# Writing four of eight memory steps of an encoder layer at another place in the instruction order

## The chip, the cores and the metric

The kernel runs on one core of a Trainium2 chip. The metric is the device time of one execution in microseconds (us). Before the change the median of three runs is 3056.3 us (3049.87 to 3058.04). One further execution was profiled; the profile's rows come from that one.

A core has five engines that run side by side, each with its own queue of instructions that it takes in order: TensorE (PE, matrix products; its weight loads are listed as PEld), VectorE (DVE), ScalarE (ACT), GpSimd (POOL) and SyncE (SP, which here only issues transfers). Transfers are carried out by 16 DMA engines that all queues share. The working memory is SBUF; products land in PSUM, from which ScalarE or VectorE copy them.

## The reference

One layer on a sequence of 2048 tokens with 1024 channels, all in 32-bit floats:

```
u    = rmsnorm(x);  P = u @ w_in                       # 1024 x 3600
hyena = long convolutions of P's first 1536 columns    # by FFT, two orders, gated
mlstm = two-way recurrence over q, k, v, o, gates      # 4 heads x 128
h    = x + concat(norm(hyena), norm(mlstm)) @ w_out
h    = h + cross_attention(rmsnorm(h), rmsnorm(mem))   # mem: 256 tokens, 4 heads x 256
h    = h + relu(rmsnorm(h) @ ff_w1)^2 @ ff_w2
out  = rmsnorm(h)
```

What matters here is the cross attention. Its scores are `(xn @ wq) . (memn @ wk)` and its output `softmax(scores) @ (memn @ wv) @ wo`, per head. The kernel forms two small matrices per head from the memory alone: `wq_h @ (memn @ wk_h)^T`, stored in DRAM as `gd` (the key step), and `(memn @ wv_h) @ wo_h`, stored as `vw` (the value step). Four heads make four key steps and four value steps. Attention later multiplies the tokens with `gd` and the softmax with `vw`, and reads both from DRAM.

## The kernel before

Tokens are taken in two halves of 1024 (`hf` 0 and 1), whose operands lie in SBUF as a high and a low part (`xh`, `xl`); a product is three matmuls of such parts (`mm3`, lines 355 to 359). The input projection consists of *sweeps* (`sweep`, 256 columns of `w_in` each, transposed result, then a width-3 convolution; columns 0 to 5 feed Hyena, 6 and 7 are q, 8 and 9 are k) and of *natural blocks* (`natural`, 256 columns, tokens in rows; blocks 0 and 1 are v, 2 and 3 are o and the gates). Each sweep and natural block takes its weights from one stream, `self.wst`, whose order is the list `items` in `inproj_open`. The stream loads one entry ahead, into tiles `wh` and `wl` of which there are two each, through smaller staging tiles `wn`, and splits them on ScalarE and VectorE (`split`, line 366).

`program` writes the instructions in this order. First come the sweeps 0 to 3 of half 0 and of half 1, woven with the generation of Hyena's filters. Then `rest` is woven with `hyena`: `weave(rest, p.hyena(hs), 445, 329)` lets both generators advance in the ratio of 445 to 329, measured by the numbers that they yield. `rest` holds the sweeps 4 to 9 of half 1, the natural blocks 3, 0, 1, 2 of half 1, and then the blocks and sweeps of half 0, among which the gate computation (`gates`) and the backward states of the recurrence (`states`) are advanced. The last ones are the sweeps 6 and 7 and the natural block 2 of half 0. Hyena has for each of two orders a forward transform (`spectrum`, writes `zs`), 16 steps (lines 956, 987, 1030: read `fs` and `zs`, write `zg` by POOL's queue), and a last stage of eight blocks, which reads `zg` and the gate rows of `hy` (lines 339 and 974) and multiplies them with small products (lines 173 and 186).

When both are through, the tiles `xh` and `xl` are given up (`turned_in`), and the memory steps (`memproj`) are written: eight times a projection (`project`, line 708, 32 products in the records) and a key or value step (line 725 or 737), of which each projection stands one step ahead. After the first projection the first five steps of the recurrence (`mlstm`) are written among them. The memory, transposed and scaled with its norm, comes from `prep_mem`, which also begins the loads of the memory weights (`raw_stream`, unsplit, up to four entries ahead). Results go from PSUM to staging tiles `st` (three, shared with sweeps and natural blocks) on ScalarE and to DRAM by POOL's queue. Then comes attention, woven with the other steps of the recurrence, and the feed-forward part.

The written order isn't the final one: the builder orders each engine's instructions itself by an estimate of their times (`schedule_with_timeline_sim=True`), with the written order as priority, except where a line pins instructions to it.

Of the kernel before, what the change touches and what calls it, by code (L numbers as in the profile page):

```python
# [128 lines left out]
class Prog:  # L129
# [249 lines left out]

    def weights(self, pool, w, n, kc=4, bufs=2, nbufs=2, pin=False):  # L380
        nc = self.nc
        kt = w.shape[0] // 128
        hi = pool.tile([128, kt, n], F32R, tag="wh", name="wh", bufs=bufs)
        lo = pool.tile([128, kt, n], F32R, tag="wl", name="wl", bufs=bufs)
        if n > 512:
            for k0 in range(kt):
                for c0 in range(0, n, 512):
                    cs = slice(c0, c0 + 512)
                    nat = self.isw.tile([128, 512], F32, tag="wn", name="wn", bufs=nbufs)
                    nc.sync.dma_start(out=nat, in_=w[128 * k0:128 * k0 + 128, cs])  # L390
                    self.split(hi[:, k0, cs], lo[:, k0, cs], nat)
            return hi, lo
        for k0 in range(0, kt, kc):
            nat = self.isw.tile([128, kc, n], F32, tag="wn", name="wn", bufs=nbufs)
            nc.sync.dma_start(out=nat, in_=w[128 * k0:128 * (k0 + kc), :].rearrange("(k p) c -> p k c", p=128))
            self.split(hi[:, k0:k0 + kc], lo[:, k0:k0 + kc], nat, pin)
        return hi, lo

    def stream(self, pool, items, cur, **kw):
        for w, n in items:  # L400
# [25 lines left out]
    def inproj_open(self, es):  # L426
        nc, tc, a = self.nc, self.tc, self.a
        self.d_hy = self.dram("hy", (3, L, CH))
        self.d_qt = self.dram("qt", (4, 128, L))
        self.d_kt = self.dram("kt", (4, 128, L))  # L430
        self.d_kn = self.dram("kn", (L, CH))
        self.d_vd = self.dram("vd", (L, CH))
        self.d_od = self.dram("od", (L, CH))
        self.d_gt = self.dram("gt", (L, 16))
        sw = self.isw = es.enter_context(tc.tile_pool(name="i_w", bufs=1))
        for tag, n, bufs in (("cv", 1088, 2), ("wn", 544, 4)):
            for _ in range(bufs):
# [24 lines left out]

# [202 lines left out]
    def prep_mem(self):  # L665
# [24 lines left out]
                yield  # L690
        self.prepq = halves()

    def memproj(self):
        nc, sb = self.nc, self.isb
        gd = self.dram("gd", (2, 128, 8, 512))
        vw = self.dram("vw", (4, 128, 8, 256))
        self.pop(2)
        mt = self.memt

        mul = nc.tensor.matmul  # L700

        def project():
            w = next(self.mst)
            p = self.mm().rearrange("p (k t) -> p k t", k=2)
            for m in range(2):
                ms = slice(128 * m, 128 * m + 128)
                for k in range(8):
                    mul(p[:, m], w[:, k, ms], mt[k // 4][:, k % 4], start=k == 0, stop=k == 7)
            t = sb.tile([128, 4, 256], F32, tag="xn", name="kt", bufs=2)[:, 0:2]
            nc.scalar.copy(t, p)  # L710
            return t

        def staged(p):
            o = self.ist.tile([128, 2, 256], F32, tag="st", name="o", bufs=3)
            nc.scalar.copy(o, p)
            return o

        def keys(h, t):
            q = next(self.mst)
            for i2 in range(4):  # L720
                p = self.mm().rearrange("p (i t) -> p i t", i=2)
                for i in range(2):
                    ds = slice(256 * i2 + 128 * i, 256 * i2 + 128 * i + 128)
                    for m in range(2):
                        mul(p[:, i], q[:, m, ds], t[:, m], start=m == 0, stop=m == 1)
                cs = slice(256 * (h % 2), 256 * (h % 2) + 256)
                nc.gpsimd.dma_start(out=gd[h // 2, :, 2 * i2:2 * i2 + 2, cs], in_=staged(p))
# [1350 lines left out]
def chain(*gens):  # L2078
    for g in gens:
        yield from g  # L2080
# [20 lines left out]
def program(p):  # L2101
    with ExitStack() as ms:
        with ExitStack() as es:
            p.inproj_open(es)
            p.filters_open()
            p.prepq = p.x_first()
            p.pop()
            s = chain(p.sweep(range(4), 0, True, lambda: p.prep_x(1)), p.opened(), p.sweep(range(4), 1, False))
            f = p.filters()
            for _ in range(5):  # L2110
                next(s)
            next(f)
            next(f)
            next(s)
            weave(s, f, 140, 102, True)
            p.gates_open(es)
            n = p.memproj()
            m = p.mlstm(ms)
            with ExitStack() as hs:
                rest = chain(s, p.sweep(range(4, 10), 1, True), p.natural(1, (3, 0, 1, 2), True),  # L2120
                             p.natural(0, (3,)),
                             paced(chain(p.sweep((4, 5, 8, 9), 0, False), p.natural(0, (0, 1))),
                                   p.gates(), back := p.states(), (0, 1) * 6 + (2,) * 6 + (2, 0)),
                             among(chain(p.sweep((6, 7), 0, False), p.natural(0, (2,), p.prep_mem, 2)), twice(back), 1),
                             )
                weave(rest, p.hyena(hs), 445, 329)
            for _ in chain(p.turned_in(), take(n, 1), beside_each(n, take(m, 5))):
                pass
        with ExitStack() as rs:
            p.ts = rs.enter_context(ExitStack())  # L2130
            p.tail_open(p.ts)
            with ExitStack() as at:
                g = p.attention(at)
                weave(g, m, 440, 112, True)
                ms.close()
                p.ffn_open(rs)
                for _ in g:
                    pass
            p.ffn()
# [68 lines left out]
```

## Time and profile before

| | |
|---|---|
| runs | 3058.04, 3056.3, 3049.87 us, median 3056.3 |
| profiled execution | 3061.91 us, its span 3060.2 us, mean granted TensorE clock 0.989 |
| busy | TensorE 2980.1 us (97%), VectorE 1943.0 (63%), ScalarE 1490.5 (49%), GpSimd 1261.1 (41%) |
| DMA | 607.03 MB, 198 GB/s over the span |

A row of the stretches gives, for a window of the span in us, its length and for each engine the busy time (and the number of instructions), then the mean granted TensorE clock (1.00 is full speed), the share of the 16 DMA engines that was busy, and GB/s. In a row by time, the first two numbers are start and duration, and a bracket gives how long the engine had been idle and what ended that. In a row of waits stand the total, the number and the longest. In a row of a line stand the shortest, median and longest duration in ns and the first and last start. In a row of a DMA issue stand the number, the size of each and, where the profile has it, the median time from issue to landing.

### The profile page before, as it was taken

The numbers are of one execution on the slowest core, as the hardware profiler recorded it, in microseconds if no ns is written. First come the engines' busy times: TensorE is split into PE (matmuls) and PEld (weight loads), VectorE is DVE, ScalarE is ACT, GpSimd is POOL, SyncE is SP. The second block draws the span as 40 slices with busy tenths as digits, with TensorE's granted clock in tenths as the row PEclk, the third lists the DMA queues.
The fourth block names the chain that finished last, engine by engine and source line by source line (L and its number), as shares of the span: only waits on it lengthen the run. The fifth ranks groups of instructions, "written<-read, shape, count | busy, mean of one in ns | idle before, by whom it ended". The sixth has DMA issues, their size and how long they took to land.

```text
span 3060.2 us, 44139 instructions
## 1 busy us (share of the span) xinstructions
PE 2980.1 (97%) x14799; PEld 2365.7 (77%) x14799; DVE 1943.0 (63%) x3442; ACT 1490.5 (49%) x2930; POOL 1261.1 (41%) x1025
## 2 busy tenths in 40 slices
PE   9999999998999899999999999999999999999998
PEld 7666667775677687788887888888888888888876
DVE  7856464566755557777665665558555686566695
ACT  6443455634664246555544455556555543333335
POOL 0112113321443754243223247765655474345653
PEclk9999999999999999999999999999999999999999
DMA  6655677686876986463657466657544655444434
GB/s 220 190 186 171 208 264 222 196 277 210 272 239 204 324 301 208 148 234 120 212 188 271 132 219 221 207 169 258 183 151 152 203 187 170 124 153 126 150 100 165
DMA packets 423643, 607.03 MB, mean 198 GB/s; under 512 B 36846, under 2 KB 229998, under 8 KB 422392
## 3 DMA queue, kind: packets, MB, share of 16 engines
q1 hardware_dynamic: 395972, 525.42, 53.6%
q0 software_dynamic: 18992, 62.96, 5.6%
q10 hardware_dynamic: 8452, 15.83, 1.4%
q8 instruction: 117, 1.92, 0.3%
q14 instruction: 110, 0.90, 0.1%
HBM read 401.67 MB, written 202.41 MB: 197 GB/s over the span
## 4 chain that ended last, share of the span: by engine, by line
PE 81%; DMA 7%; DVE 5%; issue 2%; ACT 2%; POOL 1%; SPq 1%; DVEq 0%; POOLq 0%; ACTq 0%
PE mm L355 17%; PE mm L358 17%; PE mm L359 17%; PE hy L359 6%; PE hy L355 6%; PE hy L358 6%; PE hy L173 2%; PE mm L956 2%; PE hy L1030 2%; PE hy L987 1%; DMA a<-zg 1%; PE hy L1322 1%; PE hy L1324 1%; PE hy L1200 1%; PE mm L737 1%
## 5 line engine op out<-in xcount | busy, mean ns | idle before, releaser
L1693 ACT CAST ah<-w 128x512 fp32r<-128x512 f32 x284 | 176.7, 623 | 303.8 <-PE hy L358 156.3
L1694 DVE TENSOR_TENSOR bl<-wr,bh 128x512 fp32r<-128x512 f32 x213 | 235.7, 1111 | 130.8 <-ACT bh L1693 130.7
L366 DVE TENSOR_TENSOR wl<-wn,wh 128x512 fp32r<-128x512 f32 (+1 forms) x296 | 216.9, 777 | 96.3 <-ACT wh L366 95.9
L355 PE MATMUL mm<-xh,wh 128*128 128x512 f32 x640 | 266.6, 418 | 3.7 <-ACT st L201 1.8
L358 PE MATMUL mm<-xl,wh 128*128 128x512 f32 x640 | 256.9, 401 | 4.9 <-DVE xl L366 4.8
L1693 ACT CAST bh<-wr 128x512 fp32r<-128x512 f32 x232 | 143.3, 620 | 229.2 <-PE mm L359 173.9
L359 PE MATMUL mm<-xh,wl 128*128 128x512 f32 x640 | 253.9, 397 | 0.0
L1694 DVE TENSOR_TENSOR al<-w,ah 128x512 fp32r<-128x512 f32 x236 | 214.8, 910 | 54.0 <-ACT ah L1693 53.9
L359 PE MATMUL mm<-bh,al 128*128 128x512 f32 x576 | 224.1, 392 | 3.9 <-DVE al L1694 3.9
L355 PE MATMUL mm<-bh,ah 128*128 128x512 f32 x576 | 226.2, 393 | 1.3 <-DVE acc L1855 1.2
L358 PE MATMUL mm<-bl,ah 128*128 128x512 f32 x576 | 225.4, 391 | 0.0
L366 ACT CAST wh<-wn 128x512 fp32r<-128x512 f32 (+1 forms) x296 | 164.5, 620 | 105.8 <-PE mm L359 51.4
L358 PE MATMUL mm<-act,wh 128*128 128x512 f32 x512 | 201.8, 394 | 0.0
L355 PE MATMUL mm<-act,wh 128*128 128x512 f32 x512 | 199.4, 395 | 1.4 <-ACT wh L366 1.3
L359 PE MATMUL mm<-act,wl 128*128 128x512 f32 x512 | 199.7, 392 | 0.9 <-DVE wl L366 0.9
L355 PE MATMUL hy<-bh,ah 128*128 128x512 f32 x448 | 175.2, 391 | 0.0
L358 PE MATMUL hy<-bl,ah 128*128 128x512 f32 x448 | 174.6, 390 | 0.0
L359 PE MATMUL hy<-bh,al 128*128 128x512 f32 x448 | 174.4, 390 | 0.0
L331 POOL TENSOR_TENSOR b<-b 128x512 f32<-128x512 f32 x32 | 48.1, 1505 | 295.6 <-DVE b L330 291.2
L355 PEld LDWEIGHTS mm<-xh,wh 128*128 128x128 f32 x640 | 121.4, 190 | 53.7 <-issue 19.4
L358 PEld LDWEIGHTS mm<-xl,wh 128*128 128x128 f32 x640 | 121.6, 190 | 50.6 <-issue 19.7
L355 PE MATMUL mm<-wh,xh 128*128 128x256 f32 (+1 forms) x512 | 156.5, 306 | 1.8 <-DVE a L960 1.8
(396 smaller groups left out, 8253.9 us busy)
## 6 DMA issues: line engine op xcount, KB each, us to landing
wr<-hc SPq DMA_DIRECT2D x224, 256.0 KB
w<-in_ff_w_dram SPq DMA_DIRECT2D x172, 256.0 KB
hc<-wn SPq DMA_DIRECT2D x128, 256.0 KB
wn<-in_w_in_dram SPq DMA_DIRECT2D x100, 256.0 KB
hc<-q SPq DMA_DIRECT2D x96, 256.0 KB
fs<-a SPq DMA_DIRECT2D x32, 512.0 KB
zs<-a POOLq DMA_DIRECT2D x32, 512.0 KB, 6.1
a<-fs SPq DMA_DIRECT2D x64, 256.0 KB
```

The costliest lines, as they stand in the source:

```text
L173: b = self.nc.tensor.matmul(*products[-1], start=True, stop=True)
L331: nc.gpsimd.tensor_tensor(b, f, b, ALU.subtract)
L355: first = mm(ps, lh, rh, start=start, stop=False)
L358: mm(ps, lh, rl, start=False, stop=False)
L359: self.last = mm(ps, ll, rh, start=False, stop=stop)
L366: both = (self.nc.scalar.copy(hi, src), self.nc.vector.tensor_tensor(lo, src, hi.bitcast(F32), ALU.subtract))
L737: mul(p, t[:, m, ms], o_[:, m, ds], start=m == 0, stop=m == 1)
L956: nc.tensor.matmul(pp, dm[:, m], t[:, m], start=True, stop=True)
L987: nc.tensor.matmul(pg, em[:, m], y, start=True, stop=True)
L1030: nc.tensor.matmul(pp, dm[:, m], t[:, m], start=True, stop=True)
L1693: self.nc.scalar.copy(hi, src)
L1694: eng.tensor_tensor(lo, src, hi.bitcast(F32), ALU.subtract)
```

## The change

The four key steps leave `memproj` and become a generator of their own, `memkeys`, which is written at four places of `rest`: after sweep 6, after sweep 8, after natural block 3 and after natural block 0, all of half 1. Their weights leave the list of `raw_stream` and become entries of `items`: each is a pair of `xa_wk`'s columns and `xa_wq`'s rows of one head, loaded by the new `raw_pair` straight into the two tiles `wh` and `wl` without a split. `memkeys` loads and scales the transposed memory into a pool of its own, `m_k`, once more than before (the value steps still use the copy of `prep_mem`). In a key step the projection now stands directly ahead of its products. The value steps stay where they were, now four steps beside the first three of the five steps of the recurrence. The weights 445 and 329 of the interleaving stay.

```diff
     def weights(self, pool, w, n, kc=4, bufs=2, nbufs=2, pin=False):
         nc = self.nc
+        if n is None:
+            return self.raw_pair(pool, w)
...
+    def raw_pair(self, pool, ws):
+        ts = []
+        for tag, w in zip(("wh", "wl"), ws):
+            kt, n = w.shape[0] // 128, w.shape[1]
+            t = pool.tile([128, kt, n], F32, tag=tag, name="wm", bufs=2)
+            for k0 in range(0, kt, kt // 2):
+                src = w[128 * k0:128 * k0 + 64 * kt].rearrange("(k p) c -> p k c", p=128)
+                self.nc.sync.dma_start(out=t[:, k0:k0 + kt // 2], in_=src)
+            ts.append(t)
+        return ts
...
-        mem = first[:1]
-        for i in range(8):
+        mem = first[4:5]
+        for i in range(4, 8):
             mem += first[i + 1:i + 2] + second[i:i + 1]
-        items = tr[:4] * 2 + tr[4:] + [nat[c] for c in (3, 0, 1, 2, 3)]
+        early = [((first[h][0], second[h][0]), None) for h in range(4)]
+        items = tr[:4] * 2 + tr[4:7] + early[:1] + tr[7:9] + early[1:2] + tr[9:] + nat[3:] + early[2:3]
+        items += nat[:1] + early[3:] + [nat[c] for c in (1, 2, 3)]
...
+    def memkeys(self):
+        nc, sb = self.nc, self.isb
+        gd = self.dram("gd", (2, 128, 8, 512))
+        with self.tc.tile_pool(name="m_k", bufs=1) as mk:
+            mt = [mk.tile([128, 4, 256], F32, name=f"mk{h}") for h in range(2)]
+            for h in range(2):
+                nc.sync.dma_start(out=mt[h], in_=self.a["mem_t"].rearrange("(k p) t -> p k t", p=128)[:, 4 * h:4 * h + 4])
+            rb = self.spread(self.diagonal(self.rm))
+            for k in range(8):
+                self.gained(mt[k // 4][:, k % 4], self.g_mem[:, k:k + 1], rb)
+            yield 0
+            for h in range(4):
+                w, q = next(self.wst)
+                t = sb.tile([128, 512], F32, tag="rb", name="kt", bufs=2).rearrange("p (k t) -> p k t", k=2)
+                self.mem_project(w, mt, t)
+                yield 7
+                for i2 in range(4):
+                    p = self.mm().rearrange("p (i t) -> p i t", i=2)
+                    for i in range(2):
+                        ds = slice(256 * i2 + 128 * i, 256 * i2 + 128 * i + 128)
+                        for m in range(2):
+                            nc.tensor.matmul(p[:, i], q[:, m, ds], t[:, m], start=m == 0, stop=m == 1)
+                    cs = slice(256 * (h % 2), 256 * (h % 2) + 256)
+                    nc.gpsimd.dma_start(out=gd[h // 2, :, 2 * i2:2 * i2 + 2, cs], in_=self.mem_staged(p))
+                yield 7
...
         t = project()
-        for i in range(8):
+        for i in range(4):
             yield 11
-            nxt = project() if i < 7 else None
-            (keys if i < 4 else values)(i % 4, t)
+            nxt = project() if i < 3 else None
+            values(i, t)
             t = nxt
...
-                rest = chain(s, p.sweep(range(4, 10), 1, True), p.natural(1, (3, 0, 1, 2), True),
-                             p.natural(0, (3,)),
+                k = p.memkeys()
+                rest = chain(s, p.sweep((4, 5, 6), 1, True), take(k, 3), p.sweep((7, 8), 1, True), take(k, 2),
+                             p.sweep((9,), 1, True), p.natural(1, (3,)), take(k, 2), p.natural(1, (0,)), k,
+                             p.natural(1, (1, 2), True), p.natural(0, (3,)),
```

`mem_project` and `mem_staged` are the projection and the staging copy of `memproj`, now shared by both.

More of the change, by code (lines that the diff above doesn't have):

```diff
@@ L691, in prep_mem, with mem_project, mem_staged @@
         self.prepq = halves()
+    def mem_project(self, w, mt, t):
+        p = self.mm().rearrange("p (k t) -> p k t", k=2)
+        for m in range(2):
+            ms = slice(128 * m, 128 * m + 128)
+            for k in range(8):
+                self.nc.tensor.matmul(p[:, m], w[:, k, ms], mt[k // 4][:, k % 4], start=k == 0, stop=k == 7)
+        self.nc.scalar.copy(t, p)
+        return t
+    def mem_staged(self, p):
+        o = self.ist.tile([128, 2, 256], F32, tag="st", name="o", bufs=3)
+        self.nc.scalar.copy(o, p)
+        return o
@@ new lines, in memkeys @@
+    def memkeys(self):
[6 more added lines that the diff above has]
+            rb = self.spread(self.diagonal(self.rm))
+            for k in range(8):
+                self.gained(mt[k // 4][:, k % 4], self.g_mem[:, k:k + 1], rb)
[9 more added lines that the diff above has]
+                        ds = slice(256 * i2 + 128 * i, 256 * i2 + 128 * i + 128)
+                        for m in range(2):
+                            nc.tensor.matmul(p[:, i], q[:, m, ds], t[:, m], start=m == 0, stop=m == 1)
+                    cs = slice(256 * (h % 2), 256 * (h % 2) + 256)
+                    nc.gpsimd.dma_start(out=gd[h // 2, :, 2 * i2:2 * i2 + 2, cs], in_=self.mem_staged(p))
+                yield 7
@@ L693, in memproj @@
     def memproj(self):
         nc, sb = self.nc, self.isb
-        gd = self.dram("gd", (2, 128, 8, 512))
         vw = self.dram("vw", (4, 128, 8, 256))
         self.pop(2)
-        mt = self.memt
-        mul = nc.tensor.matmul
+        mt, mul, staged = self.memt, nc.tensor.matmul, self.mem_staged
         def project():
[L703 to L708, printed above, removed]
-            t = sb.tile([128, 4, 256], F32, tag="xn", name="kt", bufs=2)[:, 0:2]
-            nc.scalar.copy(t, p)
-            return t
@@ L713, in staged @@
[L713 to L727, printed above, removed]
+            t = sb.tile([128, 4, 256], F32, tag="xn", name="kt", bufs=2)[:, 0:2]
@@ L729, in values @@
+            return self.mem_project(next(self.mst), mt, t)
         def values(h, t):
```

## The prediction

> **What bounds the kernel now.** I read the page first, then busy time by stretches, then TensorE's waits and its instructions in order of time in the worst stretch.
>
> ```profile
> span 3060.2 us, 44139 instructions
> PE 2980.1 (97%) x14799; PEld 2365.7 (77%) x14799; DVE 1943.0 (63%) x3442; ACT 1490.5 (49%) x2930; POOL 1261.1 (41%) x1025
> ```
>
> TensorE works 97% of the span. The change takes no matmul away, so what it can win is idle TensorE time (3060.2 - 2980.1 = 80.1 us in all) and matmuls that run slowly behind such a stall. The stretches show where these lie:
>
> ```profile
> core 0: us, PE busy (x) PEld busy (x) DVE busy (x) ACT busy (x) POOL busy (x), PEclk, DMA share, GB/s
> 350.00:475.00 125.00, 114.73 (x585) 77.66 (x554) 69.03 (x105) 72.97 (x118) 24.86 (x32) 0.97 0.83 279
> 475.00:625.00 150.00, 150.00 (x885) 116.45 (x883) 84.53 (x132) 90.24 (x166) 58.24 (x64) 1.00 0.64 199
> 625.00:700.00 75.00, 72.61 (x519) 53.87 (x518) 38.49 (x71) 23.88 (x43) 10.40 (x17) 1.00 0.94 299
> 700.00:750.00 50.00, 39.63 (x202) 24.39 (x201) 36.93 (x141) 21.56 (x37) 5.22 (x9) 0.87 0.61 203
> 750.00:975.00 225.00, 222.73 (x1068) 163.04 (x1067) 141.55 (x250) 131.82 (x226) 90.38 (x101) 0.99 0.72 223
> 975.00:1085.00 110.00, 96.96 (x586) 78.11 (x585) 59.04 (x166) 30.26 (x66) 65.01 (x73) 0.92 1.00 326
> 1085.00:1165.00 80.00, 79.21 (x410) 60.26 (x409) 43.81 (x144) 42.94 (x146) 49.43 (x56) 1.00 0.82 277
> ```
>
> The last three columns are the granted clock, the busy share of the DMA engines and what they moved. From 975 to 1085 the DMA engines are full (share 1.00, 326 GB/s), TensorE idles 110.00 - 96.96 = 13.0 us, and its clock is 0.92. The waits and the order of time there:
>
> ```profile
> PE hy L173 <- DMA a<-zg: 10.7, 4, 4.9
> PE mm L725 <- DMA wm<-in_xa_wq_t_dram: 3.8, 2, 3.4
> PE mm L708 <- DMA wm<-in_xa_wk_dram: 0.9, 1, 0.9
> ...
> 979.49 1.03 PE L173 MATMUL hy<-a,e 64*32 64x512 f32 x1 [2.70 <-DMA a<-zg]
> ...
> 1027.31 8.14 PE L725 MATMUL mm<-kt,wm 128*128 128x256 f32 x30 [0.48 <-DMA wm<-in_xa_wq_t_dram]
> 1035.29 2.75 PE L708 MATMUL mm<-mt,wm 128*128 128x256 f32 x12
> ...
> 1062.83 1.03 PE L173 MATMUL hy<-a,e 64*32 64x512 f32 x1 [4.88 <-DMA a<-zg]
> 1064.72 4.33 PE L708 MATMUL mm<-mt,wm 128*128 128x256 f32 x12
> ...
> 1085.64 1.95 PE L1284 MATMUL hy<-qn,kk_t 128*128 128x128 f32 x16
> 1100.50 1.05 PE L1284 MATMUL hy<-qn,kk_t 128*128 128x128 f32 x8
> ...
> 1115.32 7.07 PE L708 MATMUL mm<-mt,wm 128*128 128x256 f32 x32
> ```
>
> TensorE waits for the reads of the Hyena branch's last stage (zg) and for the key steps' own weights (xa_wk, xa_wq). All come through DMA engines that the key steps help to fill. Twelve products take 2.75 us at 1035.29 and 4.33 us at 1064.72, right behind the 4.88 us stall, and the thirty at 1027.31 take 8.14 us where 30/32 of 7.07 would be 6.63. So these two stalls cost another 1.6 + 1.5 = 3.1 us in slow matmuls. The clock of the whole stretch gives an upper bound of (1 - 0.92) x 110 = 8.8 us, part of which falls into the idle time itself. I take 6.
>
> [...]
>
> **The change part by part.** *What leaves the stretch.* Four key steps:
>
> ```profile
> L708 PE MATMUL mm<-mt,wm x256: 377/379/795, 1007.6 to 1145.6; 128*128 128x256 f32 x128
> L725 PE MATMUL mm<-kt,wm x128: 379/379/794, 1026.2 to 1095.1; 128*128 128x256 f32 x128
> L715 ACT COPY o<-mm x32: 560/585/649, 1034.3 to 1161.6; 128x512 f32<-128x512 f32 x32
> L689 DVE SCALAR_TENSOR_TENSOR mt<-xt,par,rb x8: 475/476/486, 991.4 to 994.3; 128x256 f32<-128x256 f32 x8
> ...
> wm<-in_xa_wk_dram SPq DMA_DIRECT2D x8, 512.0 KB
> wm<-in_xa_wq_t_dram SPq DMA_DIRECT2D x8, 512.0 KB
> gd<-o POOLq DMA_DIRECT2D x16, 256.0 KB, 6.6
> vd<-st POOLq DMA_DIRECT2D x16, 256.0 KB, 3.5
> xt<-in_mem_t_dram SPq DMA_DIRECT2D x2, 512.0 KB
> ```
>
> Half of L708's 256 records and all of L725's 128 belong to the keys: 256 records, at 7.07 us for 32 that is 56.6 us of TensorE. It is moved, not removed, and costs the same elsewhere. With it go 8 + 8 reads of 512 KB and 16 writes of 256 KB, 12 MB. The stretch now moves 326 GB/s x 110 us = 35.9 MB, so a third of its traffic leaves. What takes the keys' place beside the last Hyena stage is the last two sweeps and the last natural block. This follows from the weights of the interleaving: rest and Hyena are advanced at 445 to 329. The yields of the rest sum to about 451 before and 507 after (four times 14 more); Hyena's 334.8 end at 453 of those in both. So Hyena ends with the rest today and some 54 units ahead of it afterwards, and its tail has 66 units of sweeps and natural blocks around it. These read 1 MB of weights for four times 5.5 units where a key step reads 2 MB and writes 1 MB in 14.
>
> The nearest rows for such work beside Hyena at a share of 0.72 are those of 750 to 975: 2.27 us idle in 225, clock 0.99. For 350 to 700, a mean share near 0.77, it is 12.7 us in 350. Over 110 us that is 1.1 to 4.0 us. I take 3.0 us idle and 1 us of clock that stay, so the stretch gives 13.0 + 6 - 4 = **15 us**. Bounds: 0, if the Hyena reads stay as late, and 13.0 + 8.8 = 21.8.
>
> *What arrives in the middle.* Where the written places lie on the old time axis is seen from the ends of the blocks ahead of them:
>
> ```profile
> 356.78 1.27 DVE L798 SCALAR_TENSOR_TENSOR cv<-P,par,cv 128x1008 f32<-128x1008 f32 x1 [0.81 <-ACT cv L796]
> 418.40 0.68 DVE L803 TENSOR_SCALAR cv<-cv 128x1008 f32<-128x1008 f32 x1
> ...
> 503.07 0.72 POOL L896 DMA_DIRECT2D od<-st  x1 [5.33 <-ACT st L893]
> 541.48 0.73 POOL L896 DMA_DIRECT2D vd<-st  x1 [3.05 <-ACT st L891]
> ```
>
> Sweep 6 ends near 357, sweep 8 near 418, natural block 3 near 503, block 0 near 541. So two steps land in 350 to 475 (share 0.83) and two in 475 to 625 (0.64). Adding 3 MB a step at 326 GB/s is 9.2 us of full DMA; with its own 14.1 us of TensorE each, the second stretch would go from 0.64 x 150 = 96 us in 150 to 114.4 in 178, still 0.64; the first, with the second copy of the transposed memory (1 MB), from 103.8 in 125 to 125.2 in 153, 0.82. So the key steps bring as much time as traffic. Their weights are asked for one block ahead, behind the slot that the block before frees, and on SP's queue they stand ahead of Hyena's reads for the following step: if the slot is late, those are late. On POOL's queue the 16 gd writes stand among Hyena's multiplications and stores; one waits for its ScalarE copy (0.585 us), which waits for one of three staging buffers:
>
> ```profile
> ACT o L715 <- DMA gd<-o: 11.9, 4, 6.8
> ```
>
> In the full stretch a gd write takes 6.6 us to land and ScalarE stood 11.9 us for buffers; the vd writes of the same size, from the same queue and buffers in the natural blocks, take 3.5. The middle has the price of the latter. ScalarE and VectorE get relief there, since a key block needs no split. For new TensorE waits I take a quarter of the 4.7 us that the weights cost in the full stretch for each of four steps, **4 us** in all. Bounds: -5 (the stretch 350 to 475 idles 10.3 us, and key products that wait for neither ScalarE nor VectorE could fill half) and +29 (four times a 4.9 us stall with 2.4 us of slow matmuls).
>
> *What is added.* One spread matmul, two copies, two multiplications of the diagonal and eight of 0.476 us on VectorE (3.8 us): under 1 us on TensorE, the rest beside sweep work; **0.5 us**.
>
> *The turn between the two Hyena orders* (700 to 750: 10.4 us idle, clock 0.87). It now meets the gate computation on VectorE:
>
> ```profile
> L1114 DVE TENSOR_TENSOR pad<-pad 64x128 f32<-64x128 f32 x14 | 4.0, 284 | 0.4
> ```
>
> Since the rest falls behind Hyena by up to 56 units, the gates come later, against the first steps of the second order, and the turn meets natural blocks. Such small operations collide with another consumer. I count 0, bounds -10 and +10.
>
> *The start of the recurrence.* Its buffers lie where the operands xh, xl were, so it starts when the last natural block is done:
>
> ```profile
> 1007.80 1.52 DVE L1253 COPY rows<-rp 128x512 f32<-128x512 f32 x1 [0.77 <-PE mm L359]
> ...
> 1029.26 0.90 SPq L1258 DMA_DIRECT2D kk_t<-kt x1
> ...
> 1030.77 1.27 POOL L1290 TENSOR_TENSOR rw<-rw,qn 128x512 f32<-128x512 f32 x1 [6.27 <-DMA qn<-qt]
> ```
>
> Today its set-up begins at 1007.80, its second key block is asked for at 1029.26, and its first product runs at 1085.64, hidden by key work and Hyena's tail; from there on 55.8 us of memory work (32 of L725's, 96 of L708's and 64 of L737's records) lie beside its first steps. After the change the set-up of some 25 to 30 us eats half of the four value steps' 55.8 us, and the following steps have less cover, while attention's second half of the first column block waits for four of them. Four steps of 15 us (from the scores at 1085.64 to the next at 1100.50) would end about 30 + 60 = 90 us after that release, and their output goes through memory once more; TensorE has 55.8 us, four steps' own products of some 6 us each and some 10 us of attention's first half, together about 90, to do meanwhile. I take **3 us**; bounds 0 and 15.
>
> The sum: -15 + 4 + 0.5 + 0 + 3 = -7.5 us, plus what the two estimates on either side leave open. A shorter set-up than today's is likely without the full queues (POOL stood 6.27 us for qn), so I round the gain up to 9. Against the profiled execution's 3061.9 us (span 3060.2 and 1.7 around it) that is 3052.9; the median of the runs, 3056.3, lies 5.6 lower, so **3047 us**.
>
> **Rivals.** (1) *The waits only move.* Key weights or zg reads come late in the middle for as much as the tail gives: +15 in place of +4 there, 3058 us. For it: 350 to 475 already idles 10.3 us at share 0.83, and the mean traffic of the whole stretch does not fall. Against it: 475 to 625 does not idle at all at 0.64. The builder's own ordering by its time estimate could also put the key products elsewhere than written, which ends here too. (2) *All of the tail is won*, and the turn loses its collision with the gates: -21 + 2 - 8 + 1, about 3031 us. For it: 39.63 of 50 us beside 36.93 us of VectorE. Against: Hyena's own copies wait there too. (3) *The recurrence's start becomes the bound*, the slower case: set-up waits for xh and xl, and there are no key steps behind them. Its place is right behind the last natural block; its price is the 78 us from 1007.80 to 1085.64 if that delay belongs to its loads and not to its place in the order, less the 55.8 us that values and little else cover, so 22 us, with 3 us already counted: -9 + 19 is 10 slower, 3066 us. It decides from about 18 us on (9 to undo the gain, 9 to be seen). For it: its first loads wait behind others on SP's queue. Against: qn was there by 1030.77 and the second key block was asked for at 1029.26, so the order, not the loads, kept the product until 1085.64.
>
> **Numbers.** Forecast (a gain of 3 to 15 us) 0.48; rival 1, 0.20; rival 2, 0.15; rival 3, 0.17. A measurement of this kernel tells about 0.3%, 9 us, from no change. The forecast lies at that edge: a little over half of it (0.28) with rival 2 (0.15) gives 0.43 faster; the rest of it (0.20) with most of rival 1 (0.17) gives 0.37 same; rival 3 (0.17) and a worse rival 1 (0.03) give 0.20 slower. The range runs from rival 2's 3031, a little below, to rival 3's 3066: 3028 to 3067; the forecast's own is 3041 to 3053.
>
> **What would show it.** Right: the last 110 us of Hyena at a DMA share below 0.9 with under 5 us idle; L173's waits for zg in the tail gone; key products near sweep 6, sweep 8 and natural blocks 3 and 0 without waits for their weights; the 56.6 us of key work found there. Wrong: new waits for weights or zs, zg and fs reads between 350 and 700 above 10 us, a longer turn, or idle time of over 10 us between the last natural block and attention's first products.

## The result and the profile after

The changed kernel takes 3090.8 us (median of four runs, 3086.9 to 3092.9), the kernel before, measured beside it, 3054.6 us (3049.9 to 3058.0). The ratio is 1.0111, 95% interval 1.0097 to 1.0126: the change costs 36 us. The prediction was 3047 us, and its range, 3028 to 3067, doesn't hold the result. The profiled execution took 3092.94 us, 31.0 more than that of the kernel before.

The head of the page after:

```profile
span 3091.2 us, 44138 instructions
PE 2992.4 (97%) x14801; PEld 2374.8 (77%) x14801; DVE 1944.7 (63%) x3452; ACT 1494.5 (48%) x2931; POOL 1258.6 (41%) x1025
```

TensorE has two instructions more, as written, but is busy 12.3 us longer and idle 98.8 us instead of 80.1. The 31.0 us are 18.7 us of new waiting and 12.3 us of longer products. Busy time by stretches, first the kernel before, then the changed one (columns as in the prediction; of the kernel before, 750 to 975 and 975 to 1085 stand there). The parts are the sweeps with filters, the middle, the tail of Hyena, the start of the recurrence, and the rest. The last row holds the same work in both (7973 products). The middle has the same length in both, but after the change it holds the key steps and less of the rest's own work; and the tail's row after the change reaches over the recurrence's set-up into its first steps.

```profile
350.00:750.00 400.00, 376.96 (x2185) 272.37 (x2154) 228.99 (x447) 208.65 (x363) 98.72 (x121) 0.97 0.75 243
1085.00:1300.00 215.00, 207.43 (x1097) 169.78 (x1096) 148.85 (x416) 119.91 (x383) 95.49 (x92) 0.98 0.65 213
1300.00:3060.00 1760.00, 1738.01 (x7973) 1442.00 (x7971) 1126.47 (x1718) 828.45 (x1596) 862.68 (x602) 1.00 0.54 178
```

```profile
350.00:750.00 400.00, 365.63 (x2037) 264.84 (x2038) 195.69 (x319) 191.73 (x335) 102.10 (x131) 0.95 0.78 254
750.00:975.00 225.00, 215.95 (x945) 149.85 (x944) 155.75 (x331) 139.55 (x237) 75.81 (x83) 0.99 0.70 211
975.00:1150.00 175.00, 174.44 (x1055) 139.95 (x1055) 99.87 (x264) 59.54 (x126) 99.94 (x114) 1.00 0.86 276
1150.00:1331.00 181.00, 157.06 (x862) 136.31 (x861) 134.40 (x387) 101.86 (x340) 68.77 (x59) 0.92 0.53 169
1331.00:3091.00 1760.00, 1738.26 (x7973) 1442.23 (x7971) 1124.59 (x1718) 829.72 (x1596) 863.52 (x602) 1.00 0.55 178
```

Length minus busy time of TensorE gives its idle time (of the first 350 us TensorE is busy 337.99 before and 341.08 after):

| stretch | idle before | idle after | difference |
|---|---|---|---|
| 0 to 350 | 12.0 | 8.9 | -3.1 |
| middle (350 to 975) | 25.3 | 43.4 | +18.1 |
| tail (975 to 1085; 975 to 1150) | 13.0 | 0.6 | -12.5 |
| start (1085 to 1300; 1150 to 1331) | 7.6 | 23.9 | +16.4 |
| rest (1760 us in both) | 22.0 | 21.7 | -0.2 |

The clock column goes the same way: the tail rises from 0.92 to 1.00, the start falls from 0.98 to 0.92, the first part of the middle from 0.97 to 0.95. So the tail gave about the idle time that was forecast, and the start and the middle took more than that.

TensorE's waits after the change, in the middle (350 to 960, the dearest of them) and at the start (1085 to 1200):

```profile
PE hy L173 <- ACT a L1027: 4.8, 2, 3.7
PE mm L355 <- DVE sg L929: 4.8, 1, 4.8
PE hy L173 <- DVE a L1080: 4.5, 2, 3.6
PE hy L173 <- DMA a<-zg: 4.3, 1, 4.3
PE hy L1016 <- DVE b L1065: 4.2, 4, 2.6
PE mm L713 <- issue: 3.9, 1, 3.9
PE mm L985 <- DMA a<-fs: 3.8, 2, 3.6
```

```profile
PE hy L1351 <- DVE bry L213: 7.2, 1, 7.2
PE hy L1509 <- DVE act L366: 4.9, 1, 4.9
```

In neither stretch does a wait stand under the name of the key steps' weights (`wm`). Of the rows of the middle, 13.5 us are waits for Hyena's own copies and multiplications on ScalarE and VectorE (`a`, `b`), and 8.1 us are waits for its reads (`zg`, `fs`). The start waits for the recurrence's chain of small operations, and in order of time it looks so:

```profile
1087.33 0.42 DVE L1282 COPY rows<-rp 128x512 f32<-128x512 f32 x1
1126.73 1.06 PE L1229 MATMUL hy<-va,kn 128*128 128x129 f32 x8
1127.63 1.95 PE L1313 MATMUL hy<-qn,kk_t 128*128 128x128 f32 x16
1159.76 0.39 PE L1353 MATMUL hy<-cf,rw 128*128 128x129 f32 x2
1163.82 0.30 ACT L208 ACTIVATE brm<-ss,eps 128x8 f32<-128x8 f32 x1
1165.88 1.28 DVE L1323 TENSOR_TENSOR rw<-rw,hy 128x512 f32<-128x512 f32 x2
1167.31 0.77 PE L1351 MATMUL hy<-va,rw 128*128 128x129 f32 x2 [7.16 <-DVE bry L213]
1185.23 0.66 PE L1509 MATMUL hy<-ident,wn 128*128 128x128 f32 x4 [0.71 <-DVE cf L1235]
```

The last natural block is done at 1087.33, the recurrence's first scores run at 1127.63, 40.3 us later and right behind the last products of the backward states (1126.73), and attention's first transposes (L1509) at 1185.23, 57.6 us after the scores. Between 1159.76 and 1167.31 TensorE has nothing to run while ScalarE and VectorE pass small results from hand to hand.

### The profile page after: what moved, and what is told of

It is laid out like the page before. It is cut to its first block, busy times and chain, and to the rows that moved or that the text cites. A ratio compares the mean times of both kernels' runs of the same rounds, so it can differ in the third digit from the quotient of the medians.

```text
span 3091.2 us, 44138 instructions
## 1 busy us (share of the span) xinstructions
PE 2992.4 (97%) x14801; PEld 2374.8 (77%) x14801; DVE 1944.7 (63%) x3452; ACT 1494.5 (48%) x2931; POOL 1258.6 (41%) x1025
## 4 chain that ended last, share of the span: by engine, by line
PE 80%; DVE 7%; DMA 6%; issue 3%; ACT 2%; POOL 1%; SPq 1%; DVEq 0%; ACTq 0%; POOLq 0%
PE mm L355 17%; PE mm L359 17%; PE mm L358 17%; PE hy L359 6%; PE hy L358 6%; PE hy L355 6%; PE hy L173 2%; PE mm L985 1%; PE hy L1059 1%; PE hy L1016 1%; PE hy L1351 1%; PE hy L1353 1%; DVE xt L529 1%; DMA a<-zg 1%; DVE wl L366 1%
```

## The experiments

All ratios are to the kernel before, measured beside each kernel. The expectations name theories by letters, which stand for what the same sentence says. "Set-up" is the time from the end of the last natural block to the first scores, "chain" that from the first scores to attention's first transposes.

**Keys in both places, and in none.** The first kernel keeps the early key steps and writes them again where they used to be. The second has none at all; attention reads a weight in the place of `gd`.

```diff
-        mem = first[4:5]
-        for i in range(4, 8):
+        mem = first[0:1]
+        for i in range(0, 8):
...
-        for i in range(4):
+        for i in range(0, 8):
...
-            values(i, t)
+            (keys if i < 4 else values)(i % 4, t)
```

> The changed kernel, with the four key steps written a second time at their old place behind the last natural block (gd is written twice, the weights are read twice). Three theories. A, the start is bare: the changed kernel loses about 25 us at the recurrence's start, because the key steps no longer lie beside it. B, the middle: nearly all of the 36 us is lost in the middle, where the key steps now stand. C, late states: the recurrence starts late because the last backward state is written late. The doubled steps are 56.6 us of TensorE. A: the stall at the start goes, so 3091 + 56.6 - 25, 3123 us, up to 3142 if the tail's DMA is full again. B: nothing is won, 3148 us and more. C: as A, since the extra work hides the lateness too. Against the old kernel plus 56.6 us (3111 us) the rest is what the key steps cost in the middle: about 12 us by A, over 36 by B.

```diff
-        items = tr[:4] * 2 + tr[4:7] + early[:1] + tr[7:9] + early[1:2] + tr[9:] + nat[3:] + early[2:3]
-        items += nat[:1] + early[3:] + [nat[c] for c in (1, 2, 3)]
+        items = tr[:4] * 2 + tr[4:] + [nat[c] for c in (3, 0, 1, 2, 3)]
...
-                k = p.memkeys()
-                rest = chain(s, p.sweep((4, 5, 6), 1, True), take(k, 3), p.sweep((7, 8), 1, True), take(k, 2),
...
+                rest = chain(s, p.sweep(range(4, 10), 1, True), p.natural(1, (3, 0, 1, 2), True), p.natural(0, (3,)),
```

> No key steps at all: neither in the middle nor at the tail (gd isn't computed; attention reads another weight of the same size in its place). Everything else as in the old kernel. The old kernel less 56.6 us of work is 2998 us. A: the tail wins 13 to 19 us, the recurrence's start loses 25: 3004 to 3010 us, with idle time of over 15 us between the last natural block and attention. B: only the win at the tail is left, 2979 to 2985 us. C: the gates aren't late against Hyena here, so the start isn't either, 2979 to 2990 us.

Measured: both places 3116.8 us, ratio 1.0205 [1.0186, 1.0224], 62.9 over before. No key steps 3039.0 us, 0.9948 [0.9929, 0.9967], 14.9 under before. The first lies 6 us under what theory A expected and 31 under B. The second missed all three theories, by 29 us and more: 56.6 us of products are gone and the kernel is only 14.9 us faster. With the 36.2 of the change the four corners read:

| | no late key steps | late key steps | what the late ones cost |
|---|---|---|---|
| no early key steps | -14.9 | 0 | 14.9 |
| early key steps | +36.2 | +62.9 | 26.7 |
| what the early ones cost | 51.1 | 62.9 | |

The four steps are 56.6 us of products (32 of one projection take 7.07). At the old place they cost 15 to 27 us, in the middle 51 to 63. So the old place is not a burden: some 30 to 42 us of the key work there ran in time that TensorE would else have lost. Without key steps, the chain's 57 us stand bare (busy time of the set-up and of the chain; then TensorE's groups in the chain, busy time and mean, and the idle time before them):

```profile
1000.40:1075.90 75.50, 64.05 (x273) 37.58 (x272) 36.45 (x104) 19.79 (x49) 52.02 (x59) 0.95 0.96 307
1075.90:1133.00 57.10, 32.38 (x194) 29.59 (x192) 36.73 (x125) 27.20 (x106) 34.42 (x37) 0.73 0.63 197
```

```profile
L1350 PE MATMUL hy<-va,rw 128*128 128x129 f32 x64 | 15.4, 333 | 21.1 <-DVE hy L216 11.7 <-DVE ht L1384 4.0 <-ACT ht L1364 3.5
```

TensorE is busy 32.4 of 57.1 us at a clock of 0.73, nearly all of it with the recurrence's own products. With key steps in both places the start is full:

```profile
1050.00:1100.00 50.00, 49.55 (x357) 44.82 (x356) 32.36 (x95) 21.40 (x44) 28.35 (x36) 1.00 0.93 296
1100.00:1150.00 50.00, 48.89 (x270) 43.90 (x269) 17.51 (x53) 14.81 (x37) 28.42 (x36) 1.00 1.03 370
1150.00:1200.00 50.00, 50.00 (x264) 39.72 (x263) 25.30 (x96) 30.51 (x115) 29.10 (x30) 1.00 0.81 269
```

These rows also say that full DMA engines alone didn't stop TensorE here: 370 GB/s at a share of 1.03 beside 48.89 of 50 us.

Where the cover went is seen from the memory work in the chain. First the kernel before (1085.6 to 1161.3), then the changed one, in its set-up and in its chain:

```profile
L737 PE MATMUL mm<-wm,kt 128*128 128x512 f32 x64 | 28.8, 592 | 0.0
L708 PE MATMUL mm<-mt,wm 128*128 128x256 f32 x96 | 22.0, 379 | 0.0
L725 PE MATMUL mm<-kt,wm 128*128 128x256 f32 x25 | 5.9, 379 | 0.0
```

```profile
L713 PE MATMUL mm<-mt,wm 128*128 128x256 f32 x92 | 21.1, 380 | 0.0
L766 PE MATMUL mm<-wm,kt 128*128 128x512 f32 x32 | 14.1, 592 | 0.0
...
L766 PE MATMUL mm<-wm,kt 128*128 128x512 f32 x32 | 14.2, 592 | 0.0
L713 PE MATMUL mm<-mt,wm 128*128 128x256 f32 x14 | 3.2, 379 | 0.0
```

Before, 56.7 us of memory work lay beside the chain (28.8 + 22.0 + 5.9). After the change 35.2 us are used up during the set-up and 17.4 are left.

**The backward states.** They too run later after the change, and the recurrence's first steps read them from DRAM (`cbd`). The next kernel reads a part of a weight in their place, so that nothing waits for them.

```diff
-                get(out=cbn.rearrange("d h e -> d (h e)"), in_=cbd[n])
+                get(out=cbn.rearrange("d h e -> d (h e)"), in_=a["w_in"][0][0:128, 0:516])
```

> The changed kernel, but the recurrence reads the backward states' place from a weight of the same size and not from cbd (the backward states are still computed and stored, but not used). This takes away the wait of the recurrence's first steps for the last backward state, and nothing else. A: no change beyond 5 us, 3086 to 3091 us. B: no change. C: the start's stall goes, 15 to 25 us less, 3066 to 3076 us.

Measured: 3087.2 us, 1.0109 [1.0091, 1.0127]; chain 54.2 us instead of 57.6. So waiting for the states' values costs some 3 us, which the intervals don't tell from nothing. But this kernel leaves the states' products where they are: the last ones run at 1122.54 and the first scores right behind them, at 1123.43, as in the changed kernel. Whether late states hold back the scores is therefore not settled; an order that only writes the states earlier wasn't tried. The loss doesn't need them: without key steps no such product stands in the 60 us ahead of the scores, and the chain is bare all the same.

**The places.** The key steps later, behind the natural blocks 3, 0, 1 and 2 of half 1, away from the stretch with the fuller DMA engines:

```diff
+        items = tr[:4] * 2 + tr[4:] + nat[3:] + early[:1] + nat[:1] + early[1:2] + nat[1:2] + early[2:3]
+        items += nat[2:3] + early[3:] + nat[3:]
...
+                rest = chain(s, p.sweep(range(4, 10), 1, True), p.natural(1, (3,)), take(k, 3), p.natural(1, (0,)),
+                             take(k, 2), p.natural(1, (1,)), take(k, 2), p.natural(1, (2,), True), k, p.natural(0, (3,)),
```

> The changed kernel with the four key steps one place each later: behind the natural blocks 3, 0, 1 and 2 of half 1, so none stands in the stretch where DMA is full at 350 to 400 us. The runs so far give, by difference: the middle costs 26 us beside its own 56.6 us of work, the tail wins 20, the bare start costs 31. D, the places: if the middle's 26 us come from key steps in a full DMA stretch (first loads, ScalarE waiting for gd writes), this is 8 to 15 us faster than the changed kernel, 3076 to 3083 us. E, the alignment: if they come from the gates and the turn meeting other Hyena work, since the rest falls behind Hyena by 56 units, nothing changes, 3086 to 3096 us.

Measured: 3087.2 us, 1.0099 [1.0084, 1.0114], 30.8 over before where the change is 36.2 over, with intervals that overlap. The place within the middle isn't the cause.

**Fewer steps moved.** Two early and two late, then one early (behind natural block 0) and three late, the latter also with 459 in place of 445:

```diff
-            for h in range(4):
+            for h in range(2):
...
-        for i in range(4):
+        for i in range(2, 8):
...
-            values(i, t)
+            (keys if i < 4 else values)(i % 4, t)
```

> Two key steps early (behind natural blocks 3 and 0 of half 1), two at the old place. H, a hole of fixed size: between the last natural block and attention there is a hole of about 42 us that memory work fills at no cost (no key steps at all is only 15 us faster than the old kernel although 56.6 us of work is gone). Two steps of 14.15 us left at the tail fill 28 of it: 13 us are bare and the two early steps cost 28 to 31 us: 3054 - 15 + 28 = 3067 us, 3062 to 3072. B, the middle alone: half of the changed kernel's loss, 3072 us; A without a threshold says the same. Below 3060 us speaks for a hole smaller than 42.

> One key step early (behind natural block 0 of half 1), three at the old place. H: the hole is still filled, so the 14.15 us leave the tail at full worth and are paid in full in the middle: 3054 us, 3050 to 3058, the same as the old kernel, or a few us less if the tail's full DMA is relieved. Without a threshold it would be a quarter of the changed kernel's loss, 3063 us.

> As the last, with the weights of the interleaving 459 to 329, which is the old ratio for a rest that is 14 units longer. E: the gates and the turn meet the same Hyena work as in the old kernel, so the key step costs its own 14 us and no more; with H, 3046 to 3054 us. If the alignment doesn't matter, the same as the last run.

Measured: two moved 3068.8 us, 1.0036 [1.0024, 1.0049], 12.4 over before; one moved 3062.3, 1.0027 [1.0015, 1.0039], 5.8 over; one moved with 459, 3059.4, 1.001 [0.9999, 1.0021], 3.0 over. The first hit what the hole gives (13 over; half of the change's loss would be 18, outside the interval). The second lies 8 us above the hole's 3054, and near the 3063 that was expected without any threshold. The third lies 5 us above what was expected of it, and the intervals don't tell it from the second. One step costs 3 to 6 us, two 12, four 36: the last two steps taken away cost twice as much as the first two, as with a cover that runs out. But with 445 even the first one isn't free. None of the numbers tried wins anything.

**The alignment of Hyena with the rest.** The key steps make `rest` 56 units longer with the weights unchanged. The changed kernel with 501, which restores the old alignment, and later with 473:

```diff
-                weave(rest, p.hyena(hs), 445, 329)
+                weave(rest, p.hyena(hs), 501, 329)
```

> The changed kernel with the weights of the interleaving 501 to 329 in place of 445 to 329, so that Hyena is written to end with the rest again and the gates stand against Hyena's steps as in the old kernel. A: Hyena's tail lies beside the value steps and the start again; part of the stall at the start goes, 3075 to 3085 us. B: the middle keeps its key steps and their stalls, 3086 to 3096 us. C: gates and states come as early against Hyena as in the old kernel, so the start is won back, 3066 to 3080 us.

> Changed kernel with 473:329. With 445 it took 3090.8 and with 501 3093.4, the middle cleaner and the hole at the recurrence's start wider at 501. Theory (a hole of fixed length behind the set-up, which grows by as much as Hyena's end leaves uncovered): 3086 to 3095. Rival (a best alignment in between, of which the changed kernel only lacks the setting): 3065 to 3080, which would put half of the loss on alignment.

Measured: 501 3093.4 us, 1.0127 [1.0108, 1.0146]; 473 3085.3 us, 1.0094 [1.0077, 1.0111]. The first hit theory B's range, but not for its reason, that the middle would keep its stalls: at 501 the middle is the cleaner one, and the start loses what that gains (350 to 700, 700 to 750, then two windows of the start). The second lies 1 us under what the theory of a hole expected, and at least 5 above the rival, a best alignment in between:

```profile
350.00:700.00 350.00, 335.82 (x1829) 251.12 (x1828) 172.49 (x282) 183.53 (x320) 93.38 (x116) 0.99 0.75 246
700.00:750.00 50.00, 48.24 (x365) 35.11 (x363) 23.61 (x46) 15.73 (x31) 8.29 (x14) 1.00 0.84 270
...
1100.00:1150.00 50.00, 33.88 (x167) 20.83 (x166) 29.38 (x88) 10.20 (x28) 34.53 (x38) 0.83 0.69 229
1150.00:1200.00 50.00, 24.40 (x149) 22.25 (x148) 31.39 (x111) 28.54 (x113) 23.57 (x23) 0.72 0.55 180
```

From 350 to 750 TensorE idles 15.9 us where the change with 445 idles 34.4 and the kernel before 23.0; from 1100 to 1200 it idles 41.7. Neither setting brings back more than 6 us. The same weights on the old kernel, with nothing moved, on two with key steps early, and the expectations of all of them:

> The old kernel, nothing moved, with only the weights of the interleaving changed, 390 to 329 in place of 445 to 329, so that Hyena is written some 54 units ahead of the rest at its end, as in the changed kernel. E, the alignment: the middle (350 to 1000 us) shows the stalls of the changed kernel without any key step in it, 10 to 20 us more idle time than the old kernel; the tail, which keeps its key steps, stays filled. In total 3060 to 3075 us. If the middle's loss belongs to the key steps themselves, this kernel is within 5 us of the old one, or faster by part of the tail's 20 us.

> The old kernel with the weights 420 to 329: Hyena ahead by half of that. E: between the old kernel and the last run, 3056 to 3066 us. If the alignment doesn't matter and only the tail counts, 3045 to 3055 us, which would beat the old kernel.

> Old kernel, nothing moved, weights 473:329 in place of 445:329: the rest is written earlier against Hyena (its 451 units end at 314 of Hyena's 334.8, so some 21 units of Hyena, about 6%, are left with nothing beside them but the tail's memory work). Theory E (the middle's loss beyond the keys' own work is alignment: Hyena standing ahead of the rest): not slower than 0.3% (3045 to 3064), since the rest is ahead here. Rival (any departure from 445 costs, because 445 is simply fitted to this kernel, as 390 cost 14): 3062 to 3075.

> Old kernel, nothing moved, weights 501:329 (the rest's 451 units end at 296 of Hyena's 334.8, so 38 units of Hyena, over 11%, stand beside memory work only). Theory E, sides differ: the middle is as clean as in the changed kernel with 501 (about 11 us idle from 625 to 1050), but the tail has the DMA engines full for longer; 3055 to 3075. Rival (one fitted point): as far from 445 as 390 and so as dear, 3066 or more, with the loss in the middle and not in the tail.

> Two key steps early, two at the old place (as before), with the weights 473 to 329, the old ratio for a rest that is 28 units longer. E: the middle's part of the loss goes (the run with 445 idles 16 us between 750 and 950, the old kernel 2), the part of the hole stays, 3056 to 3062 us. If the alignment doesn't matter, 3066 to 3071 us again.

> The key steps at both places, with the weights 501 to 329. E: the middle costs its own 56.6 us and under 10 more, against 26 with 445; in exchange Hyena's tail stands against the memory weights again and its 20 us come back: 3054 + 56.6 + 0 to 10 = 3111 to 3121 us, with under 15 us of idle time between 350 and 1050. If the alignment doesn't matter, idle time there stays over 25 us.

| kernel | weight | us | ratio | over before |
|---|---|---|---|---|
| old | 390 | 3068.6 | 1.0045 [1.0029, 1.006] | 13.2 |
| old | 420 | 3057.7 | 1.0003 [0.9992, 1.0014] | 2.3 |
| old | 473 | 3065.8 | 1.0033 [1.0021, 1.0045] | 10.6 |
| old | 501 | 3079.3 | 1.0081 [1.0066, 1.0096] | 24.2 |
| two early | 473 | 3069.6 | 1.0046 [1.003, 1.0063] | 14.1 |
| both places | 501 | 3107.2 | 1.0174 [1.0153, 1.0195] | 51.8 |

The theory that only a Hyena standing ahead costs falls: the old kernel loses 10.6 us at 473 and 24.2 at 501 (above the theory's 3075), where the rest stands ahead, and two early steps gain nothing from 473. With key steps in both places, however, 501 gains 11 us on 445 (51.8 over before in place of 62.9), more than was expected, though 26.8 us stay idle from 350 to 1050 where under 15 were expected (42.1 with 445). The two intervals just touch. There the late steps leave 14.6 us idle from 1050 to 1300, where the changed kernel with 501 has 44.1, so not all of the middle's gain is lost again. Alignment costs on both sides of 420 to 445, but for different reasons. At 390 the middle waits for Hyena's reads (350 to 960):

```profile
PE mm L956 <- DMA a<-fs: 10.7, 4, 6.0
PE hy L1030 <- DMA a<-zs: 6.5, 1, 6.5
```

At 501 the old kernel has the hole of the changed one, with nothing moved (1100 to 1150, 1150 to 1200):

```profile
1100.00:1150.00 50.00, 36.31 (x186) 25.33 (x186) 27.12 (x84) 22.07 (x75) 34.35 (x38) 0.91 0.75 242
1150.00:1200.00 50.00, 36.47 (x208) 32.57 (x209) 35.65 (x121) 26.07 (x95) 21.05 (x19) 0.78 0.55 180
```

Its rest ends 19 us earlier than with 445 (988.6 against 1007.8) and Hyena 38 us later, so the memory work is used up beside Hyena's end and the chain stands bare: 27.2 us idle in these two rows.

## Why the prediction was wrong

**The start of the recurrence** is the step that failed. The prediction took 3 us with bounds of 0 and 15. The idle time there grew by 16.4 us and the clock fell from 0.98 to 0.92. The corners put the loss at 30 to 42 us: they count the slow products too, and measure it from kernels that keep the late steps (with keys in both places 1.6 us are idle from 1050 to 1200). Three parts of the working were off. (1) It set 90 us of work against 90 us of steps, counted from the release, the end of the last natural block; but that work is not one pool. 35.2 us of the value work run during the set-up, and beside the chain, where TensorE has only the recurrence's products, 17.4 are left. (Its count of today's cover, 55.8 us, took 32 of L725's records where the row has 25; the rows give 56.7, so this changes nothing.) (2) The set-up takes 40.3 us and not 25 to 30. (3) That "the order, not the loads, kept the product until 1085.64" agrees with the trace, but it doesn't follow that the key steps were what stood in the way. Hyena's last small products (shortest, median and longest ns, first and last start), before and after:

```profile
L186 PE MATMUL hy<-a,e x224: 589/613/1059, 639.1 to 1074.7; 64*32 64x512 f32 x112
```

```profile
L186 PE MATMUL hy<-a,e x224: 589/613/1059, 642.1 to 1095.5; 64*32 64x512 f32 x112
```

In the kernel before, the first scores come 10.9 us behind the last of these, and 77.8 behind the release. In the seventeen profiles of this case they come never earlier than 40 us behind the release and never earlier than 3 us behind Hyena's end; even without key steps the set-up takes 75.5 us, with Hyena's end 8.4 us ahead of the scores. So the key steps were not what the recurrence waited for; they were what filled that wait. What holds the scores back stays open. In the changed kernel, with keys in both places, with the states not read, with later places and with 390 on the old kernel, Hyena ends 32 to 34 us ahead of the scores, and the last products of the backward states run right ahead of them. In the others these products lie earlier, and the scores come 3 to 16 us behind Hyena's end. No run separates these two.

**Rival 3** named this place, the side and part of the mechanism (no key steps behind the set-up), with a chance of 0.17, and priced it at 22 us from the 78 us of the old set-up. The loss comes otherwise: a shorter set-up, and a chain with too little beside it. Its point against, that qn was there by 1030.77, was true and did not decide.

**The tail's 15 us** were right in size: 12.5 us less idle time and a clock of 1.00. Its reason was not. Without any key step the DMA engines are still full there (share 0.96, 307 GB/s) and 11.5 us stay idle from 1000.4 to 1075.9; with the key steps kept and others added, the tail is as clean as after the change (0.45 us idle from 975 to 1100, clock 1.00). What cleans it is that the sweeps and natural blocks now reach to Hyena's end: 67 us lay between release and Hyena's last small product before (1007.80 to 1074.7), 8 after (1087.33 to 1095.5). The old kernel with 390 shows it with no step moved. There 18 us lie between the two, the key steps stay behind them, and the row with Hyena's end is nearly full at a clock of 1.00:

```profile
950.00:1050.00 100.00, 99.36 (x616) 81.83 (x615) 68.97 (x168) 37.11 (x71) 56.99 (x62) 1.00 0.84 260
```

The 54 units of the prediction match these 59 us (67 less 8); that Hyena ends with the rest today was off by 67.

**The middle's 4 us** were too few: 18.1 us more idle from 350 to 975, and a lower clock. Waits under the name of the key weights do not appear. The other reason given, a ScalarE copy that waits for a gd write, appears once, and TensorE waits for it:

```profile
373.66 0.58 ACT L719 COPY o<-mm 128x512 f32<-128x512 f32 x1 [4.27 <-DMA gd<-o]
374.14 1.08 ACT L1027 COPY a<-hy 128x512 f32<-128x512 f32 x2
375.28 1.11 PE L173 MATMUL hy<-a,f 32*64 32x512 f32 x1 [3.74 <-ACT a L1027]
```

ScalarE stands 4.27 us for a key step's staging buffer, Hyena's copy comes behind it, and TensorE is idle for 3.74 us until that copy is done. In the median the gd writes landed in 5.5 us, between the prediction's 3.5 and 6.6. Another 3.9 us (`L713 <- issue`) lie right ahead of the first key step, at 353.51; VectorE begins to scale the memory for it at 352.93, so the added scaling, counted with the other additions at 0.5 us, is the likely reason, which the profile doesn't name. The other waits are for Hyena's copies and reads; with 501 they shrink (15.9 us idle from 350 to 750), so they hang on which steps meet. The turn between the orders, counted at 0 with bounds of 10, took 2.6 us more (13.0 us idle from 700 to 750 in place of 10.4). Which of the other meetings costs how much stays open. Taken together, the early steps cost 51 to 63 us where their own work is 56.6; that is -5.5 to +6.3 for middle and tail, against -10.5 in the sum (-15 + 4 + 0.5). This second miss is 5 to 17 us; the start's is 27 to 39 (30 to 42 less the 3).

**What would show it** worked in part. Idle time of over 10 us between the last natural block and attention was named as a sign of a wrong prediction, and it came. Waits for weights or Hyena's reads of over 10 us between 350 and 700, named as another, did not come: 4.3 for zg, 2.0 for zs and 0.3 for fs. The signs of a right one came at the tail and for the key work: in Hyena's last 110 us the DMA share is 0.80 with 0.3 us idle, the waits for zg are gone, and the key products take 58.7 us in the middle. So these signs tell that the tail was won, and not that the change wins.

## What to carry to other kernels

Before work is taken away from a place, ask what that place would be without it: make the kernel with the work left out, and if it gains far less than the work's own time (here 14.9 us for 56.6), the work was cover (it filled time in which the engine would else have waited). Count cover for a latency chain only from the moment at which the chain runs; work that can run during its set-up will be gone by then (here 35.2 us of it, with 17.4 left). A second look at the corners (in both places, in none) tells such a case with two runs, where the busy share, 97% before and after the change, tells nothing.

## What was not expected of the hardware

A stall of TensorE was followed by slow products for longer than the stall. In the changed kernel, pairs of products of one kind before and behind the 7.16 us wait:

```profile
1159.54 0.39 PE L1351 MATMUL hy<-va,rw 128*128 128x129 f32 x2
...
1168.30 0.64 PE L1351 MATMUL hy<-va,rw 128*128 128x129 f32 x2
...
1180.54 0.39 PE L1351 MATMUL hy<-va,rw 128*128 128x129 f32 x2
```

0.64 us in place of 0.39 lasts from 1167.31 to 1180.1, 12.8 us, with stalls of 0.81 and 2.12 us within. Full speed came back 5.7 us after the end of the last of these stalls (1174.38 to 1180.1), and the two stretches of work between the stalls, 2.1 us each, did not bring it. In the kernel before, a single stall of 2.70 us, with no other behind it, was followed by 6.3 us of slow products (979.49 to 985.82; products of one kind took 0.41 us there and 0.28 behind it). That the short stalls put the return off fits both; no run here tests it by itself. Such slow products made a chain of small steps dearer than its idle time: without key steps the chain's 57.1 us have a clock of 0.73.
